# Depthwise convolution by even and odd tokens, and a substitution that starts from identity minus L

## The chip, the core and the metric

The kernel runs on one core of a Trainium2 chip. The metric is the device time of one execution in microseconds (us). The engines are PE (TensorE, matrix products; PEld is its weight loads), DVE (VectorE), ACT (ScalarE), POOL (GpSimd) and SP, whose queue issues most of the DMAs. Each engine runs its own list of instructions in a fixed order and waits on semaphores for the others.

## What is computed

The reference is an encoder trunk of two layers over 1024 tokens of width 1024, all in float32. In each layer a combined projection feeds three mixers, whose outputs are joined, projected and added, and an MLP follows. Two of the mixers matter here:

```python
def conv_module(u, dw_w, dw_b, ln_w, ln_b):
    a, g = jnp.split(u, 2, axis=-1)
    h = a * jax.nn.sigmoid(g)
    h = depthwise_conv(h, dw_w) + dw_b.astype(h.dtype)     # 31 taps, 256 channels
    h = layer_norm(h, ln_w, ln_b)
    return jax.nn.silu(h)

# in chunk_gated_delta, chunks of 64 tokens, 6 heads, forward and backward:
    A = jnp.where(strict, jnp.einsum("bhncd,bhnsd->bhncs", kb, kc) * decay, 0.0)
    sol = lax.linalg.triangular_solve(A, rhs, left_side=True, lower=True, unit_diagonal=True)
```

The third mixer is a differential attention with six heads.

## The kernel before, in words

A layer runs as `w_in_phase` (the combined projection), `attention` (with the scans of the DeltaNet in between), `w_out_phase` and `mlp`. The lines of this case are all in `w_in_phase`. The projection is a list `todo` of 21 blocks of 128 columns. A block is a weight load (L177), a split of the weights into a high part by ACT (L168) and a low part by DVE (L169), 48 matmuls of 128x512 by `mm3` (L163 to L165) and an evacuation. Between the blocks the loop at L457 to L463 takes a few steps from two generators. `prep` makes ready the DeltaNet and `conv` the convolution. The last five blocks of the list (`LATE`) run later, beside the first steps of the scans.

`conv_module` has two channel tiles of 128 channels. A tile is one `tensor_scalar` (L489) and 30 `scalar_tensor_tensor` (L491) over 128x1024, each of which multiplies a shifted view by its tap and adds it to the sum `ca`.

`prep` takes the three pairs of heads (p = 0, 1, 2). `dn_a` transposes keys and queries (L652), makes sums of squares with ACT and DVE (L654, L655, L662), takes two powers of them on POOL (L670), and makes the decayed products A and Aqk (L682 to L701) with POOL, DVE, ACT and PE. `invert` then inverts the unit lower triangles of pair p. It loads 32x32 blocks of L into `Lr` and `Lp` by way of DRAM (L750, L754), and ACT transposes half of them (L755). POOL sets `Xm` to the identity (L759, L760) and runs 31 steps of forward substitution over it, each a product (`subt`, L765) and a difference (`Xm`, L766), the second waiting for the first and the next step for both. ACT transposes the result (`XT`, L768). SP stores both (L770, L771) and loads them into the diagonal blocks of `Tt` (L779), which POOL has cleared (L774). PE makes the off-diagonal blocks (L789 to L798), ACT and DVE evacuate them (L801, L802), and SP stores `Tt` (L804). The steps of `invert` for pair p are written out between those of `dn_a` for pair p + 1, and those of the last pair between the steps of `prep_v`, which transposes v and scales it by the power `rkinv` (L622). The power `rq` is read much later, in the tail of the scans (L889).

The order of instructions on each engine is not the order of the text. A planner that simulates the engines orders all of them before the kernel runs. An instruction that is written late can be placed early if its inputs and its memory are free in that simulation. `high_priority` moves weight splits and evacuations ahead. Once placed, the order is fixed.

After the last pair, SP loads the operands of the first scan steps (`dn_b`, L719 to L727) and of the first attention head (`stkE`, `vtE`, L475, L476), in that order, and attention starts.

Of the kernel before, what the change touches and what calls it, by code (L numbers as in the profile page):

```python
# [9 lines left out]
F32 = mybir.dt.float32  # L10
F32R = mybir.dt.float32r
BF16 = mybir.dt.bfloat16
AF = mybir.ActivationFunctionType
# [65 lines left out]
class K:  # L79
# [213 lines left out]
    def w_in_phase(self, l, L):  # L293
# [3 lines left out]
        with tc.tile_pool(name=f"wA{l}", bufs=1, reuse_waits=RW) as W:  # L297
# [154 lines left out]
            XN, CN, DNN = self.SL  # L452
            with tc.tile_pool(name=f"dx{l}", bufs=1, side="right", reuse_waits=RW) as X:
                self.XC = X
                prep = self.prep(l, L, X)
                conv = self.conv_module(l, L, X, up, dw, db, lw, lb)
                while todo and len(todo) > self.LATE:  # L457
                    todo.pop(0)()
                    for _ in range(XN):
                        next(prep, None)  # L460
                    if up[1] is not None:
                        for _ in range(CN):
                            next(conv, None)  # L463
                for g in (prep, conv):
                    for _ in g:
                        pass
# [16 lines left out]
    def conv_module(self, l, L, W, up, dw, db, lw, lb):  # L483
        nc = self.nc
        cas = []
        for i in range(2):
            ca = W.tile([P, S], F32, tag="ca", bufs=2, name=f"ca{l}_{i}")
            u = up[i]
            nc.vector.tensor_scalar(ca, u[:, 0:S], dw[:, i, 0:1], db[:, i:i + 1], ALU.mult, ALU.add)  # L489
            for k in range(1, TAPS):  # L490
                nc.vector.scalar_tensor_tensor(ca, u[:, k:k + S], dw[:, i, k:k + 1], ca, ALU.mult, ALU.add)  # L491
                yield
            cas.append(ca)
        for q in range(4):
            ps = self.bank("sc0", 1).rearrange("p (t k) -> p t k", k=CONV_CH)
# [90 lines left out]

    def prep(self, l, L, X):
        gi = iter(())
        for p in range(3):
            ga = self.dn_a(l, p, L, X)  # L590
            live = True
            while live:
                live = next(ga, self) is not self
                yield
                for _ in range(2):
                    next(gi, None)
            yield from gi
            gi = self.invert(l, p, self.Aset, X)
        gv = self.prep_v(l, L, X)
        live = True  # L600
        while live:
            live = next(gv, self) is not self
            yield
            for _ in range(2):
                next(gi, None)
        yield from gi

    def prep_v(self, l, L, X):

        nc = self.nc  # L610
        for p in range(3):
            while 6 + p not in self.gqdone:
                yield
            vT = X.tile([P, NT, P], F32, tag="Kt", bufs=1, name=f"vT{l}_{p}")
            nc.sync.dma_start(vT.rearrange("p t c -> p (t c)"), self.gq[6 + p])
            for mg in range(2):
                sl = slice(4 * mg, 4 * mg + 4)
                ps = self.prep_bank()
                for m in range(4):
                    nc.tensor.transpose(ps[:, m * P:(m + 1) * P], vT[:, 4 * mg + m], self.ident)  # L620
                v = X.tile([P, 4, 2, HD], F32, tag="t2", bufs=2, name=f"vs{l}_{p}_{mg}")
                nc.vector.tensor_tensor(v, ps.rearrange("p (m h e) -> p m h e", h=2, e=HD),  # L622
                                        L["rkinv"][:, sl, 2 * p:2 * p + 2].unsqueeze(3).broadcast_to([P, 4, 2, HD]), op=ALU.mult)
                nc.sync.dma_start(self.vs[sl, :, p].rearrange("m q c -> q m c"), v.rearrange("p m h e -> p m (h e)"))
                yield

    def dn_a(self, l, p, L, X):
        nc = self.nc
# [29 lines left out]
                yield  # L658
        for d in range(2):
            nc.scalar.dma_start(self.kta[d, :, :, 0, p].rearrange("m q c -> q m c"), Kt)  # L660
        sse = X.tile([P, 2, NT, 2], F32, tag="sse", bufs=1, name=f"sse{nm}")
        nc.vector.tensor_scalar(sse, ssk, 1e-6, None, ALU.add)  # L662
        rk2 = X.tile([P, NT, 2], F32, tag="rk2", bufs=1, name=f"rk2{nm}")
        nc.vector.reciprocal(rk2, sse[:, 0])
# [1 line left out]
        for d in range(2):  # L666
            nc.vector.tensor_tensor(rho[:, d], gsel(L["beta"], d), rk2, op=ALU.mult)
            nc.vector.tensor_tensor(L["kw"][:, d, :, h0:h0 + 2], rho[:, d], L["ed"][:, :, d, h0:h0 + 2], op=ALU.mult)
        for k, w, half in (("rkinv", 0, self.phalf), ("rq", 1, self.mhalf)):
            nc.gpsimd.tensor_tensor(L[k][:, :, h0:h0 + 2], sse[:, w], half.rearrange("p (a b) -> p a b", b=2), op=ALU.pow)  # L670
        A = [X.tile([P, NT, 2, CH], F32, tag=f"A{d}", bufs=1, name=f"A{nm}_{d}") for d in range(2)]
        self.Aset = A
        yield
# [62 lines left out]
    def invert(self, l, p, A, X):  # L736
# [19 lines left out]
        yield  # L756
        Xm = X.tile([P, B, B], F32, tag="Xm", bufs=1, name=f"Xm{nm}")
        XT = X.tile([P, B, B], F32, tag="Lr", bufs=2, name=f"XT{nm}")
        nc.gpsimd.memset(Xm, 0.0)  # L759
        nc.gpsimd.memset(Xm.rearrange("p a b -> p (a b)")[:, ::B + 1], 1.0)  # L760
        for j in range(B - 1):
            n, w = B - 1 - j, j + 1
            tmp = X.tile([P, 256], F32, tag="subt", bufs=1, name=f"subt{nm}_{j}")
            tv = tmp[:, 0:n * w].rearrange("p (a b) -> p a b", b=w)
            nc.gpsimd.tensor_tensor(tv, Lp[:, j + 1:, j:j + 1].broadcast_to([P, n, w]), Xm[:, j:j + 1, 0:w].broadcast_to([P, n, w]), op=ALU.mult)  # L765
# [3 lines left out]
        xi = self.xi[p % 2]  # L769
        nc.sync.dma_start(xi[0], Xm)  # L770
        nc.sync.dma_start(xi[1], XT)  # L771
        Tt = [X.tile([P, NT, 2, CH], F32, tag=f"Tt{d}", bufs=1, name=f"Tt{nm}_{d}") for d in range(2)]
        for d in range(2):
            nc.gpsimd.memset(Tt[d], 0.0)  # L774
        Ta = X.tile([P, 16, B], F32, tag="iv", bufs=2, name=f"Ta{nm}")
        for g in range(4):
            r = slice(g * B, (g + 1) * B)
# [833 lines left out]
```

## Time and profile before

| | |
|---|---|
| median of 3 runs | 2974.86 us (2972.13 to 2975.39) |
| the profiled execution | 2969.2 us |
| its span | 2967.3 us |
| mean granted TensorE clock | 0.955 of full speed |
| PE busy | 2730.7 us (92%) |
| DVE busy | 2075.6 us (70%) |
| ACT busy | 1405.4 us (47%) |
| POOL busy | 868.4 us (29%) |

The span runs from the first instruction to the last, and 1.9 us lie outside it. The stage of this case is 100 to 435 us in the first layer and 1565 to 1907 us in the second. A busy share is an average over stages with other limits: POOL is busy 29% of the span, and in this stage most of the time.

### The profile page before, as it was taken

How to read it: one execution, taken by the hardware profiler on the slowest of the kernel's cores; microseconds unless marked ns; L12 is line 12 of the kernel's file. 1: busy time of each engine (PE TensorE's matmuls, PEld its weight loads, DVE VectorE, ACT ScalarE, POOL GpSimd, SP SyncE). 2: the span in 40 equal slices, each digit the busy share in tenths (PEclk: the TensorE clock that was granted, in tenths of full speed). 3: DMA queues.
4: the chain of work that ended last, by engine and by line, in shares of the span. 5: the costliest groups of instructions: out<-in, count | busy, mean ns of one | idle time of the engine just before them, and what ended most of it. 6: DMA issues, size and time to landing. Idle time of an engine off the chain costs nothing.

```text
span 2967.3 us, 46102 instructions
## 1 busy us (share of the span) xinstructions
PE 2730.7 (92%) x17292; PEld 2189.7 (74%) x17292; DVE 2075.6 (70%) x3701; ACT 1405.4 (47%) x2468; POOL 868.4 (29%) x793
## 2 busy tenths in 40 slices
PE   8987979997999998999999689799879999989997
PEld 7865757766888886888787567577658888868886
DVE  5797317888478776777768772378974877767876
ACT  5432315677346665332554223265863566643334
POOL 2288715747000000000112986276550000000000
PEclk9988979998999999999999889799989999999999
DMA  5557785442325557665446487844332355586553
GB/s 136 153 154 207 209 190 148 130 113 81 122 93 196 208 205 295 236 210 188 152 117 141 124 243 198 212 137 122 100 119 81 110 213 200 195 322 244 204 180 117
DMA packets 415312, 504.73 MB, mean 170 GB/s; under 512 B 125401, under 2 KB 313945, under 8 KB 412786
## 3 DMA queue, kind: packets, MB, share of 16 engines
q1 hardware_dynamic: 359362, 373.92, 42.4%
q10 hardware_dynamic: 55728, 127.88, 11.3%
q8 instruction: 136, 2.23, 0.3%
q14 instruction: 86, 0.70, 0.1%
HBM read 318.01 MB, written 182.12 MB: 169 GB/s over the span
## 4 chain that ended last, share of the span: by engine, by line
PE 67%; POOL 11%; DVE 8%; DMA 8%; issue 3%; ACT 2%; SPq 1%; ACTq 0%; DVEq 0%; POOLq 0%
PE at L163 10%; PE at L164 10%; PE at L165 10%; PE sc L163 4%; PE sc L164 4%; PE sc L165 4%; POOL Xm L766 4%; POOL subt L765 3%; DVE sc L1046 2%; PE at L1044 2%; PE dt L163 2%; PE dt L164 2%; PE dt L165 2%; PE tr L1070 2%; PE dt L861 2%
## 5 line engine op out<-in xcount | busy, mean ns | idle before, releaser
L158 POOL TENSOR_TENSOR pro<-pr,mhalf 128x1 f32<-128x1 f32 x32 | 18.5, 578 | 1415.9 <-DVE pr L207 1413.1
L163 PE MATMUL at<-hTh,wh 128*128 128x512 f32 (+1 forms) x832 | 328.4, 396 | 6.7 <-ACT cp L363 6.7
L165 PE MATMUL at<-hTh,wl 128*128 128x512 f32 (+1 forms) x832 | 326.9, 394 | 6.7 <-DVE wl L169 6.7
L164 PE MATMUL at<-hTl,wh 128*128 128x512 f32 (+1 forms) x832 | 327.2, 393 | 0.0
L1049 ACT ACTIVATE sc<-sc,mx 128x1024 f32<-128x1024 f32 x192 | 220.4, 1149 | 85.2 <-DVE mx L1046 82.8
L165 PEld LDWEIGHTS at<-hTh,wl 128*128 128x128 f32 x832 | 160.8, 193 | 39.6 <-DVE wl L169 8.2
L163 PEld LDWEIGHTS at<-hTh,wh 128*128 128x128 f32 x832 | 161.3, 194 | 38.6 <-ACT cp L363 7.5
L164 PEld LDWEIGHTS at<-hTl,wh 128*128 128x128 f32 x832 | 161.2, 194 | 31.1 <-issue 0.7
L491 DVE SCALAR_TENSOR_TENSOR ca<-cu,dw,ca 128x1024 f32<-128x1024 f32 x120 | 171.3, 1443 | 0.4
L1044 PE MATMUL at<-stk 96*128 96x512 f32 x352 | 146.7, 474 | 18.4 <-DVE mx L1046 17.2
L1046 DVE CUSTOM_DVE_ANT_0 sc<-at,bias,mx 128x512 f32<-128x512 f32 x192 | 142.4, 746 | 24.9 <-PE at L1044 19.3
L1046 DVE CUSTOM_DVE_ANT_0 sc<-at,bias 128x512 f32<-128x512 f32 x192 | 130.1, 684 | 37.1 <-PE at L1044 32.0
L765 POOL TENSOR_TENSOR subt<-Lp,Xm 128x31 f32<-128x31 f32 (+15 forms) x186 | 126.6, 680 | 84.1 <-DMA Lp<-ai 50.9
L1156 ACT ACTIVATE ob<-sb 128x512 fp32r<-128x512 f32 x120 | 74.8, 626 | 156.6 <-PE tr L165 49.3
L766 POOL TENSOR_TENSOR Xm<-Xm,subt 128x31 f32<-128x31 f32 (+15 forms) x186 | 144.8, 778 | 13.0
L163 PE MATMUL at<-ob,oa 128*128 128x512 f32 x356 | 138.3, 391 | 2.1 <-ACT at L1484 2.1
L164 PE MATMUL at<-ob,oa 128*128 128x512 f32 x356 | 138.4, 389 | 0.0
L165 PE MATMUL at<-ob,oa 128*128 128x512 f32 x356 | 138.0, 389 | 0.0
L1070 PE MATMUL tr<-consts,sc 128*128 128x128 f32 x704 | 110.4, 289 | 17.3 <-DVE sc L1066 12.2
L1156 ACT ACTIVATE ob<-w2r 128x512 fp32r<-128x512 f32 x92 | 57.5, 628 | 131.6 <-PE tr L165 48.9
L169 DVE TENSOR_TENSOR wl<-wr,wh 128x1024 fp32r<-128x1024 f32 x48 | 64.9, 1353 | 76.2 <-ACT wh L168 76.2
L1074 ACT ACTIVATE aT<-tr 128x512 f32<-128x512 f32 x160 | 91.7, 592 | 39.0 <-PE tr L1070 38.6
(462 smaller groups left out, 7937.5 us busy)
## 6 DMA issues: line engine op xcount, KB each, us to landing
hd<-oa ACTq DMA_DIRECT2D x120, 512.0 KB, 5.7
oa<-hd SPq DMA_DIRECT2D x120, 512.0 KB, 4.2
w1r<-in_w_ff_dram SPq DMA_DIRECT2D x32, 1024.0 KB, 5.6
w2r<-in_w_ff_dram SPq DMA_DIRECT2D x64, 512.0 KB, 7.0
wr<-in_w_in_dram SPq DMA_DIRECT2D x50, 512.0 KB, 5.0
ld<-hd SPq DMA_DIRECT2D x98, 256.0 KB, 4.1
kta<-kta SPq DMA_DIRECT2D x32, 576.0 KB, 8.5
stk<-qk SPq DMA_DIRECT2D x66, 256.0 KB, 4.8
```

What stands on the lines that cost most here:

```text
L163: mm(ps, lhsT=lh, rhs=rh, start=first, stop=False, skip_group_check=more)
L164: mm(ps, lhsT=lh, rhs=rl, start=False, stop=False, skip_group_check=more)
L165: mm(ps, lhsT=ll, rhs=rh, start=False, stop=last, skip_group_check=more)
L491: nc.vector.scalar_tensor_tensor(ca, u[:, k:k + S], dw[:, i, k:k + 1], ca, ALU.mult, ALU.add)
L765: nc.gpsimd.tensor_tensor(tv, Lp[:, j + 1:, j:j + 1].broadcast_to([P, n, w]), Xm[:, j:j + 1, 0:w].broadcast_to([P, n, w]), op=ALU.mult)
L766: nc.gpsimd.tensor_tensor(Xm[:, j + 1:, 0:w], Xm[:, j + 1:, 0:w], tv, op=ALU.subtract)
L1044: mm(ps, lhsT=st[:, 0, t * P:(t + 1) * P], rhs=st[:, 1, ks], start=True, stop=True)
L1046: nc.vector.tensor_tensor_reduce(out=sc[:, ks], in0=ps, in1=self.bias[:, o:o + 512], scale=slope, scalar=mx[:, 0:1] if n2 else 3.0e38, op0 ...
L1049: nc.scalar.activation(sc, sc, AF.Exp, scale=-1.0, bias=mx[:, 1:2], accum_out=oS[:, t, mp:mp + 1])
L1070: nc.tensor.transpose(ps[:, k], pp[0][:, (4 * q + k) * P:(4 * q + k + 1) * P], self.ident)
L1074: nc.scalar.activation(aT[:, 4 * q:4 * q + 4, qi * P:qi * P + P], ps, AF.Copy)
L1156: self.nc.scalar.activation(h, src, AF.Copy)
```

## The change

Four things are changed.

1. The convolution is computed by even and odd tokens. With the even and the odd samples of the padded input and the even and odd taps, three filters of half the length run over 512 outputs each: the odd samples with the sum of both tap sets (into the odd outputs, and from there into the even ones), the difference of even and odd samples with the even taps (added into the even outputs), and a second difference with the odd taps (added into the odd outputs). Per channel tile that is one `tensor_scalar` and 46 `scalar_tensor_tensor` over 512 elements at every second address, two subtractions over 526 and 527 elements, and two small instructions for the tap sums.
2. `Tt` is allocated and cleared once per layer and not once per pair, since the same blocks are overwritten each time.
3. The two powers leave `dn_a`. `rkinv` of a pair is written ahead of the v of that pair in `prep_v`, and the three `rq` after it. The sums of squares keep three buffers.
4. `Xm` starts as a copy of minus L, made by ACT, with POOL setting the diagonal to one. The first of the 31 steps is thereby done, and the others take one column less.

```diff
@@ -452,6 +452,9 @@
                 self.XC = X
+                self.Tt = [X.tile([P, NT, 2, CH], F32, name=f"Tt{l}_{d}") for d in range(2)]
+                for t in self.Tt:
+                    nc.gpsimd.memset(t, 0.0)
                 prep = self.prep(l, L, X)
@@ -486,10 +489,32 @@
             u = up[i]
-            nc.vector.tensor_scalar(ca, u[:, 0:S], dw[:, i, 0:1], db[:, i:i + 1], ALU.mult, ALU.add)
-            for k in range(1, TAPS):
-                nc.vector.scalar_tensor_tensor(ca, u[:, k:k + S], dw[:, i, k:k + 1], ca, ALU.mult, ALU.add)
-                yield
+
+            H, M = S // 2, S // 2 + 15
+            xe, xo = u[:, 0::2], u[:, 1::2]
+            ye, yo = ca[:, 0::2], ca[:, 1::2]
+            h0, h1 = dw[:, i, 0::2], dw[:, i, 1::2]
+            hs = W.tile([P, 16], F32, tag="hs", bufs=2, name=f"hs{l}_{i}")
+            nc.vector.tensor_tensor(hs[:, 0:15], h0[:, 0:15], h1, op=ALU.add)
+            nc.vector.tensor_copy(hs[:, 15:16], h0[:, 15:16])
+            x1 = W.tile([P, M], F32, tag="x1", bufs=1, name=f"x1_{l}_{i}")
+            nc.vector.tensor_tensor(x1[:, 0:M - 1], xe[:, 1:M], xo[:, 0:M - 1], op=ALU.subtract)
+            nc.vector.tensor_tensor(xe, xe, xo, op=ALU.subtract)
+            yield
+            nc.vector.tensor_scalar(yo, xo[:, 0:H], hs[:, 0:1], db[:, i:i + 1], ALU.mult, ALU.add)
+            for k in range(1, 16):
+                nc.vector.scalar_tensor_tensor(yo, xo[:, k:k + H], hs[:, k:k + 1], yo, ALU.mult, ALU.add)
+                if k % 2:
+                    yield
+            nc.vector.scalar_tensor_tensor(ye, xe[:, 0:H], h0[:, 0:1], yo, ALU.mult, ALU.add)
+            for k in range(1, 16):
+                nc.vector.scalar_tensor_tensor(ye, xe[:, k:k + H], h0[:, k:k + 1], ye, ALU.mult, ALU.add)
+                if k % 2:
+                    yield
+            for k in range(15):
+                nc.vector.scalar_tensor_tensor(yo, x1[:, k:k + H], h1[:, k:k + 1], yo, ALU.mult, ALU.add)
+                if k % 2:
+                    yield
             cas.append(ca)
@@ -608,7 +634,12 @@
         nc = self.nc
+
+        def root(k, w, half, p):
+            nc.gpsimd.tensor_tensor(L[k][:, :, 2 * p:2 * p + 2], self.sse[p][:, w], half.rearrange("p (a b) -> p a b", b=2), op=ALU.pow)
+
         for p in range(3):
+            root("rkinv", 0, self.phalf, p)
             while 6 + p not in self.gqdone:
                 yield
@@ -623,6 +654,8 @@
                 yield
+        for p in range(3):
+            root("rq", 1, self.mhalf, p)
@@ -666,8 +699,7 @@
-        for k, w, half in (("rkinv", 0, self.phalf), ("rq", 1, self.mhalf)):
-            nc.gpsimd.tensor_tensor(L[k][:, :, h0:h0 + 2], sse[:, w], half.rearrange("p (a b) -> p a b", b=2), op=ALU.pow)
+        self.sse[p] = sse
@@ -756,10 +788,10 @@
-        nc.gpsimd.memset(Xm, 0.0)
+        nc.scalar.activation(Xm, Lp, AF.Copy, scale=-1.0)
         nc.gpsimd.memset(Xm.rearrange("p a b -> p (a b)")[:, ::B + 1], 1.0)
-        for j in range(B - 1):
-            n, w = B - 1 - j, j + 1
+        for j in range(1, B - 1):
+            n, w = B - 1 - j, j
@@ -769,9 +801,7 @@
-        Tt = [X.tile([P, NT, 2, CH], F32, tag=f"Tt{d}", bufs=1, name=f"Tt{nm}_{d}") for d in range(2)]
-        for d in range(2):
-            nc.gpsimd.memset(Tt[d], 0.0)
+        Tt = self.Tt
```

## Rows read from the trace of the kernel before

**Rows 1.** Page, chain of work that ended last, shares by engine
```profile
PE 67%; POOL 11%; DVE 8%; DMA 8%; issue 3%; ACT 2%; SPq 1%; ACTq 0%; DVEq 0%; POOLq 0%
```

**Rows 2.** Busy us per engine in 10 us stretches: PE, PEld, DVE, ACT, POOL, clock, DMA share, GB/s
```profile
210.00:220.00 10.00, 6.55 (x38) 5.00 (x37) 10.00 (x9) 2.23 (x3) 9.45 (x8) 0.91 1.05 258
220.00:230.00 10.00, 0.00 (x0) 0.00 (x0) 3.89 (x4) 0.00 (x0) 9.06 (x13) 0.50 0.03 11
230.00:240.00 10.00, 4.11 (x23) 3.39 (x24) 4.13 (x5) 5.00 (x5) 3.86 (x11) 0.50 0.62 170
...
400.00:410.00 10.00, 1.08 (x8) 0.92 (x8) 0.00 (x0) 0.00 (x0) 1.99 (x2) 0.62 1.05 297
```

**Rows 3.** Timeline of PE, both layers: start, us, what, idle before and releaser
```profile
235.89 1.97 PE L696 MATMUL tr<-kq 64*64 64x128 f32 x18 [17.98 <-ACT sq L654]
...
1708.20 2.46 PE L696 MATMUL tr<-kq 64*64 64x128 f32 x32 [16.74 <-ACT sq L654]
```

**Rows 4.** Timeline of ACT in the first layer
```profile
233.41 1.94 ACT L768 ACTIVATE XT<-Xm 128x1024 f32<-128x1024 f32 x1 [16.65 <-POOL Xm L766]
235.25 0.58 ACT L654 ACTIVATE sq<-tr 128x512 f32<-128x512 f32 x1
235.73 1.05 ACT L168 ACTIVATE wh<-wr 128x1024 fp32r<-128x1024 f32 x1
```

**Rows 5.** Timeline of POOL in the first layer
```profile
28.61 0.97 POOL L759 MEMSET Xm<- 128x1024 f32 x1
...
107.78 3.38 POOL L670 TENSOR_TENSOR rkinv<-sse,phalf 128x16 f32<-128x16 f32 x1
...
155.56 1.03 POOL L765 TENSOR_TENSOR subt<-Lp,Xm 128x31 f32<-128x31 f32 x1 [26.21 <-DMA Lp<-ai]
...
165.24 3.73 POOL L670 TENSOR_TENSOR rkinv<-sse,phalf 128x16 f32<-128x16 f32 x1
168.55 3.13 POOL L670 TENSOR_TENSOR rq<-sse,mhalf 128x16 f32<-128x16 f32 x1
...
203.70 1.62 POOL L766 TENSOR_TENSOR Xm<-Xm,subt 128x256 f32<-128x256 f32 x1
...
206.99 1.55 POOL L766 TENSOR_TENSOR Xm<-Xm,subt 128x255 f32<-128x255 f32 x1
208.61 1.50 POOL L765 TENSOR_TENSOR subt<-Lp,Xm 128x252 f32<-128x252 f32 x1
...
233.13 0.25 POOL L766 TENSOR_TENSOR Xm<-Xm,subt 128x31 f32<-128x31 f32 x1
...
288.15 0.95 POOL L774 MEMSET Tt<- 128x1024 f32 x1
...
343.73 0.74 POOL L766 TENSOR_TENSOR Xm<-Xm,subt 128x256 f32<-128x256 f32 x1
```

**Rows 6.** Timeline of DVE in the first layer
```profile
137.86 6.05 DVE L491 SCALAR_TENSOR_TENSOR ca<-cu,dw,ca 128x1024 f32<-128x1024 f32 x5
...
207.93 1.68 DVE L491 SCALAR_TENSOR_TENSOR ca<-cu,dw,ca 128x1024 f32<-128x1024 f32 x1
...
238.80 0.75 DVE L426 SCALAR_TENSOR_TENSOR qkl<-at,consts,qkh 128x512 fp32r<-128x512 f32 x1
239.46 1.28 DVE L491 SCALAR_TENSOR_TENSOR ca<-cu,dw,ca 128x1024 f32<-128x1024 f32 x1
```

**Rows 7.** DVE groups by line, 100 to 330 us: count, busy us, mean ns
```profile
L491 DVE SCALAR_TENSOR_TENSOR ca<-cu,dw,ca 128x1024 f32<-128x1024 f32 x60 | 86.0, 1450 | 0.2
L169 DVE TENSOR_TENSOR wl<-wr,wh 128x1024 fp32r<-128x1024 f32 x14 | 19.4, 1385 | 2.2 <-ACT wh L168 2.2
```

**Rows 8.** The chain that ended last, in order of time, end of the first layer's stage
```profile
396.65 8.02 DMA kta<-kta
...
423.39 10.49 DMA vtE<-av
433.93 1.97 PE tr L973 x8
```

More of the change, by code (lines that the diff above doesn't have):

```diff
@@ L588, in prep @@
         gi = iter(())
+        self.sse = {}
         for p in range(3):
@@ L660, in dn_a @@
             nc.scalar.dma_start(self.kta[d, :, :, 0, p].rearrange("m q c -> q m c"), Kt)
-        sse = X.tile([P, 2, NT, 2], F32, tag="sse", bufs=1, name=f"sse{nm}")
+        sse = X.tile([P, 2, NT, 2], F32, tag="sse", bufs=3, name=f"sse{nm}")
         nc.vector.tensor_scalar(sse, ssk, 1e-6, None, ALU.add)
```

## The prediction

> **What bounds the kernel now.** I read the chain that ended last, then the stage of the change in 10 us stretches, then the timelines of PE, ACT, POOL and DVE around the largest hole. PE carries 67% of the chain and POOL 11% [rows 1], although POOL is busy for only 29% of the span. So in one stage POOL takes PE's place, and that is the stage in which `invert` runs. PE does nothing at all from 220 to 230 us of the first layer while POOL is 91% busy, and little from 400 to 410 us [rows 2].
>
> The first hole is 17.98 us long, and the second layer has its twin of 16.74 us [rows 3]. Both end at `sq` on ACT. ACT had been idle for 16.65 us in front of `XT`, which waits for the last substitution step on POOL, and `sq` stands behind `XT` in ACT's fixed order [rows 4]. The planner had expected that step sooner. So the substitution of pair 0, from 155.56 to 233.38 us [rows 5], is late by its whole excess, and PE pays for it one to one. SP waits for the same step with the store of `Xm`, and the next pair's loads stand behind that, so the three substitutions of a layer follow each other. The last one leads to the hole at 400 us: `Tt` is stored, then the loads of the scans and of attention follow on one queue until `vtE` lands at 433.88 us [rows 8], while the DMA engines are full (share 1.05) [rows 2].
>
> Why is POOL late? The same difference over 256 elements takes 0.74 us at 343.73 and 1.62 us at 203.70 [rows 5]. At 203.70 DVE is full of convolution taps, which take 1.68 us there and 1.20 us undisturbed (five in 6.05) [rows 6]. In that stretch POOL's steps start 1.62 us apart [rows 5], about one tap and a little: the two engines take turns. In the POOL timeline 76 of the 372 steps of both layers are of this slow kind (22, 12 and 3 in the pairs of the first layer, 22, 14 and 3 in the second), each slower by 0.88 us (1.62 less 0.74).
>
> **Part 1, the convolution.** Before, a layer has 60 taps at 1.20 us and two openings at some 0.7: 73.4 us of DVE. After, it has 92 taps over 512 elements. The trace has no tap at every second address. The nearest row is a `scalar_tensor_tensor` over 512 elements at adjacent ones, after which the next instruction starts 0.66 us later (238.80 to 239.46) [rows 6]. I take that, since a step of two is near to a step of one. With four subtractions over as many elements at the same price, two openings at 0.4 and four small ones at 0.2 (estimates by their size), the sum is 60.7 + 2.6 + 0.8 + 0.8 = 64.9 us, a gain of 8.5 us of DVE a layer. The bounds: below, nothing excludes a tap at 0.6, half the price of the long one (5 us better). Above, a tap could cost its whole stretch of 1024 addresses, 1.20 us; ACT's transposing read takes 1.94 us against 1.05 for as many adjacent elements [rows 4]. Then a layer takes some 114 us, 41 more than before. Most taps fill time that PE does not wait for, so I count 1 us of the gain.
>
> [...]
>
> **What shorter taps do to POOL.** A POOL step that meets a tap waits for at most what is left of it. A tap shorter by 0.54 us (1.20 less 0.66) makes the wait shorter by up to 0.54. Taps are 86.0 us of DVE from 100 to 330 us [rows 7]; other lines with two inputs that also block add some 46 us in the same view, the weight splits 19.4 of them [rows 7]. So 65% of the slow steps gain: 76 x 0.65 x 0.54 = 27 us, 13 us a layer, of which 7.7 in pair 0. The lower bound is nothing, if each of the now more numerous taps catches a step that was free before; the upper is all of the 0.88, 67 us in both layers.
>
> **Part 2, the clears.** Of six clears of `Tt` a layer four fall between the substitution steps of pairs 1 and 2, at 0.95 us each [rows 5]: 3.8 us a layer go from POOL's path. The two that stay are placed early, where POOL idles. Nothing comes instead.
>
> **Part 3, the powers.** A power of 16 elements takes 3.13 to 3.73 us [rows 5], six a layer. Two stand inside the substitution of pair 0 (165.24 and 168.55) and two in that of pair 1. The change writes them later, but the planner doesn't keep the order of the text: the clear of `Xm` was placed at 28.61 us, far ahead of its lines, and the clear of `Tt` at 288.15, written behind the whole substitution, stands in the middle of it [rows 5]. Both went in as soon as their inputs and memory were free, between two steps that wait for each other. A power needs only its sum of squares, so I expect pairs 1 and 2 where they are now, at no gain. The pair at 107.78 stands ahead of `R` of pair 0; there a later rank lets `R` go first, and I take 2 us of at most 7. Bounds elsewhere: 13 us a layer off pairs 0 and 1 if the powers fall into POOL's idle time (26.21 us ahead of 155.56 [rows 5]); 7 us more if all six land in pair 2. `vs` (L622) newly waits for `rkinv` in DVE's order, with the evacuations behind it; at nothing, since POOL is free often enough ahead of it.
>
> **Part 4, the copy.** A pair loses its first step (0.25 us twice and two gaps of 0.07) and 9% of the elements, 5456 to 4960 in each of the two kinds. From 0.25 us for 31 to 0.74 for 256 [rows 5] an element is 2 ns: 2.0 us. It gains an ACT copy of 1.05 us [rows 4], the diagonal and two hand-overs, 1.6 us, on the path now, since it needs `Lp`. Net 1.0 us a pair, 3 a layer. ACT also waits for the second half of `Lp` with weight splits behind it: up to 4 us a pair if the loads are late, nothing where `XT` held ACT anyway. I take nothing and keep the 4 for the range.
>
> **The sum.** In pair 0 the path shortens by 7.7 + 1.0 + 2 = 10.7 us; a hole of 17.98 us is there to take it, so all counts. Pairs 1 and 2 shorten by 5.3 + 3.8 + 2.0 = 11 us. Of these I let half count, 5.5 us: the projection's matmuls fill PE for most of 240 to 400 us, and the loads at the end are bound by full DMA engines too. With the 1 us of DVE that is 17 us a layer and 34 us in both. Against the profiled execution, 2969.2 us, that gives 2935; the median of the runs is 5.7 us higher, and from it the forecast is 2974.9 - 34 = 2941 us.
>
> **The rivals.** *The powers do leave the path.* For it: POOL's idle time before pair 0. Then 6.6 us more in pair 0 and half of 6.6 in pair 1, 10 us a layer: 2921 us. With pairs 1 and 2 counted in full it is 2910.
>
> *The change does little.* PE and SP have fixed orders too. If the planner, which did not foresee the waits of POOL, now sets `XT` and the store of `Xm` earlier by as much as its own picture of the substitution shrinks, the hole in front of `sq` stays, and only the end of the stage gains the 11 us of pairs 1 and 2 at a quarter: some 3 us a layer, 2969 us. Against it: steps and clears are short in that picture, and the excess comes from the waits.
>
> *Slower: taps at every second address at full price.* At 1.20 us a tap DVE has 41 us more a layer, in a stretch where it is full until 220 us [rows 2]. It idles some 12 us from 220 to 240 [rows 2] and about as much up to 300, so 17 us are left over, and POOL meets taps as long as before and more of them. Less the 6 us of clears and copy that is 11 us a layer at least, and with the waits of POOL up to 20: 2997 to 3015, 3005 us in the middle. DVE breaks even at (73.4 - 4.2) / 92 = 0.75 us a tap, the kernel at about 0.95. Against it: a step of two is nearer to one than to ACT's step of 32.
>
> **How the numbers follow.** The forecast has 0.50, the powers' rival 0.16, the little one 0.15, the slow taps 0.10. The rest, 0.09, is a new wait out of the fixed orders, the 4 us of ACT on all six pairs above all: 2941 + 24 = 2965 and upward, mostly slower. A measurement of this kernel tells 0.2% from no change, 6 us. Faster: all of the first two, some of the others: 0.72. Within 0.2%: 0.10. Slower: 0.18. The range takes in the powers' rival and the little one, and of the slow taps nothing beyond 2988: 2905 to 2988. The slow end left out is about 0.13, the fast one 0.05.
>
> **What would show it.** A tap at 0.66 us and slow steps at about 1.1 us in place of 1.62; four clears gone; powers still between the steps of pairs 0 and 1; a pair of about 64 us in place of 78 for pair 0; the hole in front of `sq` below 9 us in each layer; attention starting 15 to 20 us earlier in each. Taps near 1.2 us, or a hole of the old length, would make the prediction wrong.

## The result and the profile after

| | before | after |
|---|---|---|
| median of four runs | 2974.62 us (2972.13 to 2975.39) | 2937.51 us (2935.04 to 2947.79) |
| the profiled execution, its span | 2969.2, 2967.3 us | 2935.04, 2933.2 us |
| mean granted TensorE clock | 0.955 | 0.964 |
| PE busy | 2730.7 us | 2726.0 us |
| span less PE busy | 236.6 us | 207.2 us |

The ratio is 0.9885, with a 95% interval from 0.9864 to 0.9905: 34 us less, as forecast (the medians are 37 us apart). In the two profiled executions PE idles 29.4 us less and is busy 4.7 us less, for the same matmuls at a slightly higher granted clock. The first line of the page after, and its chain of work that ended last (POOL had 11% before [rows 1]):

```profile
PE 2726.0 (93%) x17292; PEld 2178.5 (74%) x17292; DVE 2068.9 (71%) x3781; ACT 1411.7 (48%) x2472; POOL 813.4 (28%) x767
...
PE 66%; POOL 10%; DMA 8%; DVE 8%; issue 5%; ACT 2%; SPq 2%; ACTq 0%; DVEq 0%; POOLq 0%
```

Where the idle time went is seen by stage. These are the windows of before, from 100 us (first layer) and from the layer's first matmul (second layer) to the first matmul on `vtE`; columns as in [rows 2]:

```profile
100.00:433.90 333.90, 271.68 (x2144) 216.15 (x2143) 196.22 (x267) 96.48 (x125) 213.86 (x242) 0.89 0.68 184
...
1491.00:1906.90 415.90, 354.74 (x2580) 285.24 (x2579) 239.81 (x352) 141.57 (x192) 220.86 (x253) 0.90 0.63 169
```

And those of after, with three stretches of 10 us that answer to [rows 2]:

```profile
100.00:415.50 315.50, 269.42 (x2148) 214.22 (x2146) 191.99 (x304) 100.14 (x129) 190.28 (x231) 0.91 0.72 197
...
1469.30:1862.50 393.20, 345.91 (x2578) 277.11 (x2578) 236.84 (x393) 141.26 (x193) 197.72 (x240) 0.94 0.64 177
...
220.00:230.00 10.00, 2.74 (x13) 1.93 (x11) 2.40 (x5) 3.46 (x3) 9.14 (x15) 0.90 0.32 105
230.00:240.00 10.00, 5.41 (x19) 4.09 (x19) 8.07 (x15) 6.26 (x6) 5.07 (x3) 0.59 1.18 215
...
400.00:410.00 10.00, 5.40 (x50) 3.71 (x47) 2.17 (x6) 2.53 (x4) 5.84 (x5) 0.50 1.03 256
```

PE's idle time (length less the second number) falls from 62.2 to 46.1 us in the first stage and from 61.2 to 47.3 in the second. These two stages hold the whole gain. Their lengths alone mislead: they are 18.4 and 22.7 us shorter, 41 us in all, and the end moves by 34. In the second, 8.8 us of the difference is PE busy time (354.74 to 345.91) for as many matmuls (2580 and 2578 records), at a granted clock of 0.94 in place of 0.90. It is given back: behind the mark the same matmuls take 1010.7 us where they took 999.6. The stretch from 220 to 230 us is still nearly empty.

Inside a stage, idle time went in two places. These are the stretches of the first layer through the hole behind pair 0, and from 390 us to the mark, of before and then of after:

```profile
100.00:240.00 140.00, 111.98 (x597) 89.23 (x597) 118.93 (x144) 48.48 (x60) 93.71 (x84) 0.87 0.55 148
390.00:433.90 43.90, 24.76 (x213) 19.37 (x211) 6.39 (x21) 5.37 (x10) 13.60 (x12) 0.72 0.99 224
...
100.00:240.00 140.00, 117.22 (x634) 93.34 (x632) 121.61 (x185) 54.56 (x65) 91.25 (x86) 0.93 0.63 165
390.00:415.50 25.50, 15.12 (x165) 10.76 (x163) 4.99 (x14) 4.82 (x9) 9.48 (x10) 0.60 1.01 228
```

PE's idle time falls from 28.0 to 22.8 us in the first stretch, and from 19.1 to 10.4 in the last, where before PE mostly waits for the loads of the scans and of attention. In the second layer it falls from 30.4 to 21.3 us through the hole (1491 to 1712 us before, 1469.3 to 1694 after), and from 15.5 to 10.8 at the end (from 1862 us before and 1835 after). Of the 30 us, some 14 are won by the end of the hole and some 13 at the end of the stage.

The hole behind pair 0 is now shorter and stands elsewhere. In the timeline of PE, the rows that answer to [rows 3], with two smaller holes of the first layer that wait for DVE:

```profile
177.46 1.96 PE L728 MATMUL tr<-kq 64*64 64x128 f32 x21 [4.55 <-DVE Aqk L733]
...
234.59 0.28 PE L819 MATMUL dt<-Ta,Ao 32*32 32x32 f32 x2 [11.86 <-DMA Ta<-xi]
...
263.46 1.83 PE L728 MATMUL tr<-kq 64*64 64x128 f32 x21 [6.63 <-DVE Aqk L733]
...
1689.60 0.28 PE L819 MATMUL dt<-Ta,Ao 32*32 32x32 f32 x2 [10.23 <-DMA Tt<-xi]
```

The large hole was 17.98 and 16.74 us in front of `tr<-kq`, and is 11.86 and 10.23 us in front of the first matmul of the inversion, which waits for pair 0's result on its way through DRAM. POOL, in the first layer, against [rows 5]:

```profile
162.08 3.35 POOL L639 TENSOR_TENSOR rkinv<-sse,phalf 128x16 f32<-128x16 f32 x1
165.39 4.04 POOL L639 TENSOR_TENSOR rq<-sse,mhalf 128x16 f32<-128x16 f32 x1
...
203.31 0.97 POOL L798 TENSOR_TENSOR Xm<-Xm,subt 128x238 f32<-128x238 f32 x1
204.36 1.67 POOL L797 TENSOR_TENSOR subt<-Lp,Xm 128x234 f32<-128x234 f32 x1
...
207.83 0.96 POOL L798 TENSOR_TENSOR Xm<-Xm,subt 128x228 f32<-128x228 f32 x1
208.87 1.44 POOL L797 TENSOR_TENSOR subt<-Lp,Xm 128x220 f32<-128x220 f32 x1
...
225.77 0.25 POOL L798 TENSOR_TENSOR Xm<-Xm,subt 128x30 f32<-128x30 f32 x1
225.97 2.90 POOL L639 TENSOR_TENSOR rkinv<-sse,phalf 128x16 f32<-128x16 f32 x1
```

The powers of pair 1 still stand inside pair 0 (162.08 and 165.39). Those of pair 2 have left pair 1's substitution for the gap right behind pair 0 (225.97). A step that meets a tap takes about 0.96 us where it took 1.5 to 1.6. In the first layer 37 steps took over 1.2 us before, 22 of them beside a long tap. After, 16 do, each beside longer work of DVE: a weight split, or `cacc`, another and much shorter convolution on the projections of the DeltaNet:

```profile
140.22 0.75 DVE L515 SCALAR_TENSOR_TENSOR ca<-x,dw,ca 128x512 f32<-128x512 f32 x1
140.88 0.75 DVE L511 SCALAR_TENSOR_TENSOR ca<-cu,dw,ca 128x512 f32<-128x512 f32 x1
...
207.23 1.07 DVE L506 SCALAR_TENSOR_TENSOR ca<-cu,hs,ca 128x512 f32<-128x512 f32 x1
208.22 1.65 DVE L371 SCALAR_TENSOR_TENSOR cacc<-cp,cw,cacc 128x1024 f32<-128x1024 f32 x1
```

The tap at 207.23 goes with the step of 0.96 us, the `cacc` of 1024 elements at 208.22 with the step of 1.44. Undisturbed, a tap at every second address takes 0.66 us from start to start (140.22 to 140.88).

In the groups of DVE from 60 to 330 us, where 60 long taps took 86.0 us at 1450 ns [rows 7], 90 of the 92 short ones take 82.3:

```profile
L511 DVE SCALAR_TENSOR_TENSOR ca<-cu,dw,ca 128x512 f32<-128x512 f32 x30 | 27.6, 920 | 0.0
L506 DVE SCALAR_TENSOR_TENSOR ca<-cu,hs,ca 128x512 f32<-128x512 f32 x30 | 27.4, 915 | 0.2
L515 DVE SCALAR_TENSOR_TENSOR ca<-x,dw,ca 128x512 f32<-128x512 f32 x30 | 27.3, 911 | 0.0
```

So DVE is hardly less busy with the convolution: much of what it saves is paid back beside POOL. Of the 92 short taps of the first layer 65 run beside work of POOL and last 0.98 us on average, the other 27 last 0.75 (before, 47 of 60, at 1.50 and 1.27 us).

### The profile page after: what moved, and what is told of

Its sections match the earlier page's. It is cut to its first block, busy times and chain, and to the rows that moved or that the text cites. A ratio compares the mean times of both kernels' runs of the same rounds, so it can differ in the third digit from the quotient of the medians.

```text
span 2933.2 us, 46131 instructions
## 1 busy us (share of the span) xinstructions
PE 2726.0 (93%) x17292; PEld 2178.5 (74%) x17292; DVE 2068.9 (71%) x3781; ACT 1411.7 (48%) x2472; POOL 813.4 (28%) x767
## 4 chain that ended last, share of the span: by engine, by line
PE 66%; POOL 10%; DMA 8%; DVE 8%; issue 5%; ACT 2%; SPq 2%; ACTq 0%; DVEq 0%; POOLq 0%
PE at L163 10%; PE at L164 10%; PE at L165 10%; PE sc L163 4%; PE sc L164 4%; PE sc L165 4%; POOL subt L797 4%; POOL Xm L798 4%; DVE sc L1076 2%; PE at L1074 2%; PE dt L163 2%; PE dt L164 2%; PE dt L165 2%; PE tr L1100 2%; PE dt L891 2%
## 5 line engine op out<-in xcount | busy, mean ns | idle before, releaser
L1076 DVE CUSTOM_DVE_ANT_0 sc<-at,bias,mx 128x512 f32<-128x512 f32 x192 | 142.0, 745 | 19.7 <-PE at L1074 15.2
L797 POOL TENSOR_TENSOR subt<-Lp,Xm 128x30 f32<-128x30 f32 (+9 forms) x180 | 124.1, 689 | 12.5
L1100 PE MATMUL tr<-consts,sc 128*128 128x128 f32 x704 | 112.8, 291 | 12.8 <-DVE sc L1096 8.7
L798 POOL TENSOR_TENSOR Xm<-Xm,subt 128x30 f32<-128x30 f32 (+9 forms) x180 | 119.5, 664 | 13.0
L1094 POOL TENSOR_TENSOR sc<-sc,sc 128x1024 f32<-128x1024 f32 x40 | 101.7, 2543 | 27.0 <-ACT sc L1091 26.2
```

Source lines behind the costliest of these rows:

```text
L798: nc.gpsimd.tensor_tensor(Xm[:, j + 1:, 0:w], Xm[:, j + 1:, 0:w], tv, op=ALU.subtract)
L1076: nc.vector.tensor_tensor_reduce(out=sc[:, ks], in0=ps, in1=self.bias[:, o:o + 512], scale=slope, scalar=mx[:, 0:1] if n2 else 3.0e38, op0 ...
L1094: self.lastpool = nc.gpsimd.tensor_tensor(pp[0], pp[0], pp[1], op=ALU.add)
L1100: nc.tensor.transpose(ps[:, k], pp[0][:, (4 * q + k) * P:(4 * q + k + 1) * P], self.ident)
```

## The experiments

All ratios are to the kernel before on the same chip, with the 95% interval; "us" is the median. Pair 0 and pair 1 are the first layer's times from the first to the last step of the substitution. "Hole" is PE's largest idle stretch behind pair 0, in both layers; a smaller one that may follow it is not in the column.

| kernel | us | ratio | pair 0, pair 1 | hole |
|---|---|---|---|---|
| before | 2974.6 | 1 | 77.8, 67.5 | 18.0, 16.7 |
| after | 2937.5 | 0.9885 (0.9864 to 0.9905) | 69.3, 51.5 | 11.9, 10.2 |
| conv_only | 2935.5 | 0.9881 (0.9844 to 0.9918) | 72.3, 57.2 | 8.0, 8.1 |
| parts_2_to_4 | 2958.7 | 0.9957 (0.9943 to 0.9971) | 73.0, 57.4 | 17.6, 16.8 |
| taps_halved | 2972.9 | 1.001 (0.9988 to 1.0031) | 74.9, 70.8 | 10.1, 12.2 |
| unit_stride | 2942.6 | 0.9900 (0.9862 to 0.9937) | 69.3, 51.4 | 11.9, 10.6 |
| conv_padded | 2952.6 | 0.9937 (0.9916 to 0.9958) | 72.2, 62.1 | 7.8, 7.1 |
| fewer_long_taps | 2955.6 | 0.9946 (0.9927 to 0.9964) | 78.0, 62.4 | 18.0, 15.9 |
| powers_only_out | 2978.7 | 1.0014 (0.9998 to 1.0029) | 74.2, 64.4 | 14.7, 14.3 |
| powers_out | 2935.1 | 0.9877 (0.9855 to 0.9899) | 62.2, 55.4 | 10.9, 10.0 |
| copy_back | 2947.7 | 0.9913 (0.9891 to 0.9935) | 72.4, 55.5 | 8.0, 8.3 |
| clears_back | 2938.8 | 0.9881 (0.9860 to 0.9902) | 69.5, 52.7 | 11.6, 10.1 |
| third_filter_out | 2935.6 | 0.9874 (0.9854 to 0.9894) | 84.8, 41.0 | 16.5, 12.5 |
| third_out_powers_out | 2931.2 | 0.9844 (0.9827 to 0.9861) | 63.1, 41.7 | 12.8, 14.9 |

### The convolution alone, and everything else alone

The first is the kernel before with the new `conv_module` and nothing else.

> The kernel before with the convolution by even and odd tokens alone; powers, clears and the first step stay as they were. Theory (a tap of half the length keeps POOL's substitution steps waiting for less): the prediction's own terms give 7.7 + 2.7 + 1 us a layer, so some 23 us less than before, 2952 us; contended steps near 0.95 us, pair 0 near 71 us in place of 77.8, pair 1 near 61 in place of 67.5. Rival 1 (only the 8.5 us of DVE work a layer that go away count, beside a PE that doesn't wait for them): 2968 to 2974 us. Rival 2 (the clears, the powers and the copy carry the gain): 2970 us or more, pairs as before.

The second is the changed kernel with the old taps:

```diff
-            for k in range(1, 16):
-                nc.vector.scalar_tensor_tensor(yo, xo[:, k:k + H], hs[:, k:k + 1], yo, ALU.mult, ALU.add)
...
+            for k in range(1, TAPS):
+                nc.vector.scalar_tensor_tensor(ca, u[:, k:k + S], dw[:, i, k:k + 1], ca, ALU.mult, ALU.add)
```

> The changed kernel with the convolution of before (60 long taps a layer); clears once a layer, powers written later, substitution on a copy. Theory (the taps are the larger half): 2958 to 2964 us, steps that meet a tap still near 1.6 us, pair 0 near 75 us, pair 1 near 58. Rival 2 (clears, powers and copy carry it all): 2938 to 2945 us. If the parts add, this one's gain and that of the convolution alone sum to 37 us.

The convolution alone makes the whole gain, 35 us where 23 were expected; parts 2 to 4 alone make 13, within what was expected. Together they are worth 34, not 48: they seem not to add, though the 14 us between are about what the three intervals together leave open. Pair 0 of the convolution alone came as expected (72.3 us for 71), pair 1 did better (57.2 for 61), since its new order puts the powers of pair 2 outside pair 1, although its code writes them where the kernel before does. With parts 2 to 4 alone, where they are written later, they leave pair 1 in the first layer (244.13 us) and stay in it in the second. The two kinds of change differ in the hole. In the timeline of PE of the kernel with parts 2 to 4:

```profile
234.06 1.97 PE L706 MATMUL tr<-kq 64*64 64x128 f32 x22 [17.63 <-ACT sq L665]
...
1702.09 2.24 PE L706 MATMUL tr<-kq 64*64 64x128 f32 x30 [16.82 <-ACT sq L665]
```

and of the kernel with the convolution alone:

```profile
230.97 0.79 PE L163 MATMUL at<-hTh,wh 128*128 128x512 f32 x1 [8.04 <-DVE qkl L426]
...
1697.71 0.28 PE L811 MATMUL dt<-Ta,Ao 32*32 32x32 f32 x2 [8.13 <-DMA Ta<-xi]
```

Parts 2 to 4 shorten pair 0 by 4.8 us in the first layer, and the hole stays. The convolution shortens it by 5.5, and the hole falls by 10 (a second one of 3.8 us follows it; the two together are as long as the hole of the changed kernel).

### Is it the length of a tap, or the work of DVE?

```diff
-                nc.vector.scalar_tensor_tensor(ca, u[:, k:k + S], dw[:, i, k:k + 1], ca, ALU.mult, ALU.add)
+                for o in (0, S // 2):
+                    nc.vector.scalar_tensor_tensor(ca[:, o:o + S // 2], u[:, k + o:k + o + S // 2], dw[:, i, k:k + 1], ca[:, o:o + S // 2], ALU.mult, ALU.add)
```

> The kernel before with each of its 60 scalar_tensor_tensor taps a layer written as two over 512 adjacent outputs: the work of DVE doesn't shrink, it grows by 120 x 0.66 less 60 x 1.20, 7 us a layer. Theory (the length of one tap is what POOL waits for): faster than before by most of the convolution's share, 2953 to 2960 us, contended steps near 0.95 us. Rival 1 (less DVE work is what counts): 2975 to 2990 us, no gain.

The theory's 2953 to 2960 us was wrong: nothing was gained. The group of DVE from 60 to 330 us says a part of why:

```profile
L492 DVE SCALAR_TENSOR_TENSOR ca<-cu,dw,ca 128x512 f32<-128x512 f32 x120 | 105.7, 922 | 0.0
```

Half a tap lasts 922 ns in this company, where 660 had been counted, so DVE has 19.7 us more in the first layer, not 7. The groups of POOL over the whole span:

```profile
L767 POOL TENSOR_TENSOR Xm<-Xm,subt 128x31 f32<-128x31 f32 (+15 forms) x186 | 135.6, 729 | 12.8
L766 POOL TENSOR_TENSOR subt<-Lp,Xm 128x31 f32<-128x31 f32 (+15 forms) x186 | 132.8, 714 | 84.8 <-ACT cp L363 26.6 <-DMA Lp<-ai 25.6 <-DMA Ta<-xi 9.1
```

Together 268.4 us in both layers. Those of the kernel with the convolution alone:

```profile
L788 POOL TENSOR_TENSOR Xm<-Xm,subt 128x31 f32<-128x31 f32 (+15 forms) x186 | 132.9, 714 | 12.9
L787 POOL TENSOR_TENSOR subt<-Lp,Xm 128x31 f32<-128x31 f32 (+15 forms) x186 | 124.9, 671 | 72.4 <-DMA Lp<-ai 52.0 <-DMA Ta<-xi 5.6 <-ACT Lp L777 1.4
```

take 257.8 us, and 271.4 is the same sum in the kernel before (144.8 and 126.6). With 120 halves, more steps meet a tap: in pairs 0 and 1 of the first layer 68 steps take over 0.8 us, against 42 before and 56 with the convolution alone. The hole does shrink, and PE idles 15 us less than before. But PE is busy 22.7 us more with the same matmuls, at a mean granted clock of 0.950 in place of 0.955. That clock is the lowest of this kernel's ten executions (0.950 to 0.959), so the busy time is not that of a typical one, and why the shorter idle time gained nothing in the median stays open. The first line of its page, with a span of 2975.0 us:

```profile
PE 2753.4 (93%) x17292; PEld 2202.0 (74%) x17292; DVE 2113.2 (71%) x3821; ACT 1405.6 (47%) x2466; POOL 859.0 (29%) x793
```

Two kernels then separate length and work. One leaves four of the 31 taps of each tile out of the kernel before (`range(1, TAPS - 4)`).

> The kernel before with 27 of the 31 taps in each channel tile, so 54 long instructions a layer and not 62; four taps are left out, and the output is not the convolution's. DVE has 9.6 us less a layer, about as much as the convolution by even and odd tokens saves (8.5), and each tap keeps its 1.20 us. Rival 1 (less DVE work is what gains): 2938 to 2950 us, as much as the convolution alone. Theory (length of a tap): as only 13% of the taps are gone, 2962 to 2972 us.

The other adds 13 repeats of taps over `x1` a layer to the convolution alone:

```diff
+                for _ in range(2 if k < 6 + i else 1):
                     nc.vector.scalar_tensor_tensor(yo, x1[:, k:k + H], h1[:, k:k + 1], yo, ALU.mult, ALU.add)
```

> The convolution alone by even and odd tokens with 13 more half-length taps a layer (repeats of taps over x1, so the output is not the convolution's): DVE's undisturbed work is back at that of before, 73.5 us a layer, in taps of 0.66 us. Theory (length of a tap): within 8 us of the convolution alone, 2935 to 2945 us. Rival 1 (less DVE work): the gain is gone, 2965 us or more. In between, near 2950: both count about alike.

Both came out between the two readings, at 16 us less (0.9946) and 19 us less (0.9937). The groups of DVE from 60 to 330 us, of the kernel with fewer long taps (52 against 60):

```profile
L491 DVE SCALAR_TENSOR_TENSOR ca<-cu,dw,ca 128x1024 f32<-128x1024 f32 x52 | 76.0, 1476 | 0.2
```

and of the padded one:

```profile
L513 DVE SCALAR_TENSOR_TENSOR ca<-x,dw,ca 128x512 f32<-128x512 f32 x43 | 41.0, 955 | 0.2
L508 DVE SCALAR_TENSOR_TENSOR ca<-cu,dw,ca 128x512 f32<-128x512 f32 x30 | 28.6, 952 | 0.1
L503 DVE SCALAR_TENSOR_TENSOR ca<-cu,hs,ca 128x512 f32<-128x512 f32 x30 | 27.6, 922 | 0.2
```

10.0 us less of DVE (86.0 less 76.0) gave 8 us a layer, 0.8 for one. The padding brings DVE from 83.5 us (29.5, 27.1 and 26.9 in the same groups of the convolution alone) to 97.2 and takes back 8 us a layer, 0.6 for one. So work of DVE in this stage does count, at 0.6 to 0.8 us for each; the intervals of the ratios leave 0.5 to 1.1 for the first price and 0.1 to 1.1 for the second. And the padded kernel is still 19 us faster than before with 11 us more of DVE a layer: that part comes from the shorter taps and the order that goes with them. The halved taps do not fit well: by these prices they should have gained a little (19 us, less 0.6 to 0.8 times the 8.5 us by which DVE is busier than in the padded kernel, in two layers: 5 to 9 us), and their interval ends at a gain of 4.

### The stride

```diff
-            xe, xo = u[:, 0::2], u[:, 1::2]
-            ye, yo = ca[:, 0::2], ca[:, 1::2]
+            xe, xo = u[:, 0:M], u[:, M:2 * M]
+            ye, yo = ca[:, 0:H], ca[:, H:S]
```

> The changed kernel with the even and odd views replaced by the two contiguous halves of the same tiles, so every tap has as many elements at adjacent addresses; its output is not the convolution's. Theory (a step of two addresses costs DVE nothing and holds POOL no longer): within 6 us of the changed kernel, 2931 to 2944 us, taps 0.65 to 0.66 us at the least and near 0.77 in the median. Rival (a strided tap reads more lines of memory and keeps POOL out longer): contended steps under 0.85 us and 2925 us or less.

Nothing moves: the intervals of both kernels lie over each other, and the group of DVE that took 920 ns takes as long:

```profile
L511 DVE SCALAR_TENSOR_TENSOR ca<-cu,dw,ca 128x512 f32<-128x512 f32 x30 | 27.5, 917 | 0.0
```

### The powers

```diff
+            with self.tc.issue_after(self.lastXm[p - 1].ins) if p else ExitStack():
                 nc.gpsimd.tensor_tensor(L[k][:, :, 2 * p:2 * p + 2], self.sse[p][:, w], ...)
```

This was put into the changed kernel:

> The changed kernel, with the powers of pairs 1 and 2 tied behind the last substitution step of the pair before, so that POOL makes them in the 14 us in which it waits for the next pair's loads. Theory (what is inside pair 0's substitution delays PE one to one): pair 0 shorter by its two powers, 7 us, to 63 us; a hole of 11.9 and 10.2 us is there to take it, so 7 us a layer and 14 in both, 2923 us. Rival (PE's hole after pair 0 is bound by something else by now, the transfers of the pair's result or other work): pair 0 shorter by 7 us, the time within 6 us of 2937.

and, with the powers written late, into the kernel before:

> The kernel before with part 3 alone, done so that it holds: powers of pairs 1 and 2 behind the last step of the pair before; long taps, clears and first step as before. Rival 2 in its sharpest form (the gain of the convolution alone is due to the powers that leave pair 1 with the new order): 7 us less in pairs 0 and 1 of each layer, 2945 us or less. Theory (taps and powers both count, the hole in front of sq takes what pair 0 gains): 2952 to 2960 us. Third reading, from the kernel with parts 2 to 4 alone, where pair 0 got 4 us shorter and the hole stayed at 17 us: 2962 us or more.

The first had the rival's result: pair 0 is 7.1 us shorter (62.2 for 69.3) and the time the same. Attention in the first layer starts 14.4 us earlier (401.1 for 415.5 us), but PE idles only 6.0 us less up to there: 85 matmuls fewer stand ahead of that mark. In its timeline of PE the hole is hardly smaller, and in front of `sq` again:

```profile
221.58 1.97 PE L729 MATMUL tr<-kq 64*64 64x128 f32 x18 [10.91 <-ACT sq L688]
...
1673.92 2.47 PE L729 MATMUL tr<-kq 64*64 64x128 f32 x32 [9.96 <-ACT sq L688]
```

The second gained nothing either, with pairs 0 and 1 shorter by 3.6 and 3.1 us and the hole by 3.3 and 2.4. So the powers that left pair 1 don't by themselves carry the gain of the convolution.

### One part undone at a time

The step that the copy saves, put back (`memset` of `Xm`, 31 steps):

> The changed kernel with part 4 undone: identity set by POOL, 31 steps, no copy by ACT. The prediction's own count (a pair gains 2.0 us and pays 1.0, half of it counted in pairs 1 and 2): 3 to 4 us slower, 2941 us. Rival (the hand-over by ACT costs more than the first step saves; between pairs 0 and 1 the copy started 3.4 us after its input was ready, behind weight splits and an exponential): 4 us a pair back, 2927 to 2934 us.

The clears, put back into each pair:

> The changed kernel with part 2 undone: two clears of Tt in each pair, two of them between the steps of pairs 1 and 2 each time. The prediction's count (3.8 us a layer, half counted): 4 us slower, 2941 us. Rival (parts 2 to 4 add nothing once the convolution is changed, as the kernel with the convolution alone suggests): within 3 us of the changed kernel, 2934 to 2941 us; these two can be told apart only if the intervals allow it.

Without the copy the kernel is at 0.9913, 8 us more than 0.9885 would give; the intervals overlap, and the kernel with the convolution alone, which has no copy either, is at 0.9881. So it is not shown that the copy helps on top of the rest. The rival, that the kernel is faster without it, has no support. But the hand-over to ACT has a cost: between pairs 0 and 1 of the first layer POOL's substitution pauses for 14.8 us with the copy (226.0 to 240.9 us) and for 11.0 without, and pair 2 ends at 347.3 us in both. In the timeline of ACT after, the copy for pair 1 starts 3.4 us behind the end of its input:

```profile
233.71 2.02 ACT L787 ACTIVATE Lp<-Lr 64x1024 f32<-64x1024 f32 x1 [4.21 <-DMA Lr<-ai]
...
239.10 1.04 ACT L791 ACTIVATE Xm<-Lp 128x1024 f32<-128x1024 f32 x1
```

The clears make no difference that can be told (0.9881).

### Much less work, and a new order

The last two leave the third filter out of the changed kernel (30 taps a layer); the second also has the powers tied.

> The changed kernel without the third filter of the convolution, so 30 taps of 0.66 us a layer are left out, 19.8 us of DVE; its output is not the convolution's. If work of DVE in this stage counts as in the two kernels before (17 to 19 us in all for 8.5 to 9.6 us a layer, so about one to one in each layer): 40 us less, 2900 us. If only the waits of POOL count (a third fewer taps to meet, 3 to 5 us a layer): 2927 to 2932 us. If PE's own order and the transfers are the bound by now: 2931 us or more.

> The changed kernel without the third filter of the convolution, as in the run before (its output is not the convolution's), and with the powers of pairs 1 and 2 tied behind the last step of the pair before. It asks why 19.8 us less of DVE a layer gained nothing. If the new order took it back (four powers and ten steps of R and De stood inside pair 0, which took 84.8 us, and DVE idled 8.1 us for POOL's R with the last taps queued behind it while PE waited 16.5 us for those taps): pair 0 near 62 us, that hole under 6 us, 20 to 26 us less than without the tie, 2910 to 2916 us. If DVE's work has stopped counting since PE's order and the transfers are the bound: pair 0 shorter too, but the time 2930 us or more.

Without 30 taps nothing was gained, where 0.6 to 0.8 us for each of some 28 us of DVE a layer would be over 30. Pair 1 fell to 41.0 us, since no tap is left beside it, but pair 0 rose to 84.8. Its timelines of POOL, DVE and PE, first layer:

```profile
221.40 2.89 POOL L639 TENSOR_TENSOR rkinv<-sse,phalf 128x16 f32<-128x16 f32 x1
224.26 2.90 POOL L639 TENSOR_TENSOR rq<-sse,mhalf 128x16 f32<-128x16 f32 x1
...
228.62 2.42 DVE L715 TENSOR_TENSOR R<-R,consts 128x512 f32<-128x512 f32 x2 [8.14 <-POOL R L714]
230.96 0.90 DVE L511 SCALAR_TENSOR_TENSOR ca<-cu,dw,ca 128x512 f32<-128x512 f32 x1
...
235.49 0.47 PE L528 MATMUL sc<-consts,ca 128*128 128x128 f32 x1 [16.54 <-DVE ca L511]
```

The new order has pair 2's powers inside pair 0 as well. POOL's `R` comes behind them, DVE waits 8.14 us for it with the last taps queued behind, and PE waits 16.54 us for those taps. With the powers tied, pair 0 is at 63.1 us as foreseen and that hole is gone. The time falls by 9 us (0.9844), not by the 20 to 26 expected, and the two intervals just overlap: PE's hole is back in front of the inversion:

```profile
228.92 0.31 PE L820 MATMUL dt<-Ta,Ao 32*32 32x32 f32 x2 [12.83 <-DMA Ta<-xi]
...
1693.12 0.28 PE L820 MATMUL dt<-Ta,Ao 32*32 32x32 f32 x2 [14.89 <-DMA Ta<-xi]
```

So the order took back a part. No version with the whole convolution was found that is clearly faster than the changed kernel.

## Why the prediction was right, point by point

**The total was right, its parts were not.** 34 us were forecast and 34 came; that the errors of the parts cancel is luck. The forecast put some 23 us on the convolution (7.7, half of 5.3 and 1, in two layers) and 11 on the rest. The convolution alone gives 35, the rest alone 13, and beside the convolution nothing that the total shows. By place: 10.7 us a layer were counted on the hole behind pair 0 and 5.5 behind it; PE's idle time fell by 5.2 and 9.1 us in the two layers up to the end of the hole, and by 8.7 and 4.7 us at the end of the stage.

**The price of a tap: right for one alone, wrong in company.** The row chosen, 0.66 us from start to start, is what an undisturbed strided tap takes, and no cost of the stride shows (920 ns with it, 917 without, on average). But beside work of POOL a tap lasts 0.98 us on average in the first layer, and 0.75 elsewhere, and of the 8.5 us of DVE that the sum expected a layer, 3.7 at most are seen in the groups of the first layer (86.0 to 82.3, with two taps and the differences of the samples still to add).

**"I count 1 us of the gain": mis-sized.** Work of DVE in this stage was said to fill time that PE does not wait for. It counts 0.6 to 0.8 us for each, by two experiments of opposite sign. That is no price for any amount: the kernel without the third filter has some 28 us less a layer and gained nothing. PE's smaller holes wait for what is queued among the taps: `qkl` (8.04 us at 230.97, above) with the convolution alone, `Aqk` (4.55 us at 177.46 and 6.63 at 263.46) in the kernel after.

**What shorter taps do to POOL: right mechanism, half the size.** Steps that meet a tap fell to 0.96 us, better than the 1.1 foreseen. But the shorter taps took 13.6 us off the steps of both layers (271.4 to 257.8), not 27, and the stated lower bound is what happened to the halved taps: 3 us, with more slow steps (68 for 42, above). In the trace after, a step and the tap or `cacc` beside it are both longer: the step of 0.96 us at 207.83 (0.63 undisturbed, at 333.43) goes with a tap of 1.07 (0.75 undisturbed, at 140.22), the one of 1.44 at 208.87 (0.59, at 319.94) with a `cacc` of 1.65 (1.28, at 152.36).

**Pair 0 "counts one to one": wrong.** This is the step that failed in kind. In the changed kernel by itself it looks nearly right: pair 0 ends 7.4 us earlier in the first layer (233.4 to 226.0) and its hole is 6.1 us shorter. The experiments show that it is no rule. With long taps the hole is 14.3 to 18.0 us in all eight cases of the table, while pair 0 takes 71 to 78 us in these (both layers counted). With short taps, and the whole convolution, it is 7.1 to 12.2 us, while pair 0 takes 62 to 75. Parts 2 to 4 take 4.8 us off pair 0 and leave the hole; tying the powers in the changed kernel takes off 7.1 us and 1.0 of the hole; halving the taps takes off 2.9 us and 7.9 of the hole. Nor does the time follow the hole. The halved taps, and the powers tied in the kernel before, have shorter holes and gain nothing; fewer long taps gain 16 us with holes of 18.0 and 15.9.

One reading is that of the rival "the change does little": the planner knows the work and not the waits, so taking away work that is in POOL's list moves PE's list forward with it, and taking away waits does not. With the powers tied, PE does reach its hole 12 us earlier than in the changed kernel (210.7 for 222.7 us). But the same tie in the kernel before moved work out of pair 0 too, and there the hole shrank; the halves took away few waits, and it shrank by more. No trace shows the planner's own times, so the reading is not shown, and what sets the length of the hole stays open. The two kernels without the third filter are outside the pattern, at 12.5 to 16.5 us.

**The powers: half right.** Those of pair 1 stayed in pair 0, as forecast. Those of pair 2 left pair 1 (225.97 us). With that, the clears, the copy and the shorter waits, pair 1 alone is 16 us shorter, where 11 had been counted for pairs 1 and 2 together. Writing them later was not needed for it: with the convolution alone they leave in both layers, with parts 2 to 4 alone in one. The rival's price, 10 us a layer if they leave, is refuted: tied outside, they bring nothing measurable.

**The signs named beforehand.** Tap 0.66 us: yes. Slow steps 1.1: 0.96. Four clears gone: yes. Pair 0 at 64: 69.3. Hole below 9: 11.9 and 10.2. Attention 15 to 20 us earlier in each layer: 18.4, and 22.7 in the second, 8.8 of it a shorter PE busy time that is given back behind that mark.

**What stays open.** How much of the convolution's 35 us is the length of its taps and how much the order that came with them. Every edit gave a new order on all engines, and none of the experiments held it fixed. Also open are why the halved taps gain nothing and what sets the length of the hole.

## What to carry to other kernels

When two engines hold each other up, the price of an instruction is the one it has in company: a tap that lasts 0.75 us alone lasted 0.98 beside POOL here, and splitting the long instructions with no less work gained nothing. Where a planner fixes the order, the largest hole is not the price of what stands in front of it: 7 us of powers taken off the busiest chain changed nothing, and holes got shorter with no gain in time and stayed with a gain of 16 us. Add up the idle time of the whole stage, end included, and undo the parts one at a time. An engine that is 70% busy over the kernel can still be worth 0.6 to 0.8 us for each of its own in the one stage where it is nearly full (91% busy from 100 to 200 us before), as long as the new order does not take it back.

## What was not expected of the hardware

The taps over 512 fp32 elements took as long at every second address as at adjacent ones (0.66 us from start to start undisturbed, 920 against 917 ns on average). In the mean of a layer's taps, many of them beside POOL, two halves of a tap cost 2 x 922 ns where the whole costs 1450, so the split is 27% dearer there; undisturbed it is 1.32 against 1.20 us, 10%.
